# A hybrid attention and MLP layer: two more blocks of modulation columns as products on PE, page halves on ACT, and the last two fillers in one generator

## The chip, the cores and the metric

The kernel runs on one core of one Trainium2 chip. The metric is the device time of one execution in microseconds (us). The engines are named as in the profile: PE (TensorE, matrix products; PEld is its weight load), DVE (VectorE), ACT (ScalarE), POOL (GpSimd), SP (SyncE, which issues the DMAs here).

## The reference

One layer over 1024 rows of 1024 columns, in float32. A conditioning vector c gives six rows of 1024 (shift, scale and gate of two sub-layers); the mixer runs two attention groups beside each other, and an MLP with a causal convolution follows.

```python
mod = jnp.dot(jax.nn.silu(c), w_ada[l]) + b_ada[l]
sh_a, sc_a, g_a, sh_m, sc_m, g_m = jnp.split(mod, N_MOD, axis=-1)
h = modulate(rmsnorm(x, g_attn_norm[l]), sh_a, sc_a)
proj = jnp.dot(h, w_in[l])                       # q latent 256, kv latent 128, rope key 32, 3 x 512
q = jnp.dot(rmsnorm(q_lat, ...), w_q_up[l])      # 8 heads of 96
kv = jnp.dot(rmsnorm(kv_lat, ...), w_kv_up[l])   # 8 heads of 64 + 64
o_mla = mla_attention(q, k, v)                   # chunk-causal, after QK norm and rotary
o_ca = chunk_attention(cq, ck, cv, rel_bias[l])  # 9-chunk key band, 8 heads of 64
mixed = jnp.dot(jnp.concatenate([o_mla, o_ca], axis=-1), w_out[l])
x = x + g_a[:, None, :] * mixed
h = modulate(rmsnorm(x, g_mlp_norm[l]), sh_m, sc_m)
u = causal_dwconv(jnp.dot(h, w_up[l]), conv_w[l], conv_b[l])
gate, val = jnp.split(u, 2, axis=-1)
x = x + g_m[:, None, :] * jnp.dot(jax.nn.silu(gate) * val, w_down[l])
```

## The kernel before

Every product of two float32 matrices is made of three products of halves: each operand is split into a high part (a rounded copy, `hi_of`, L77) and a low part (the difference, `lo_of`, L86), and `gemm3` (L206) adds high × high, high × low and low × high in PSUM (L211 to L213). A page is a tile that holds a high and a low half.

**The opening (L298 to L513).** The eight row blocks of x are loaded, normalised in place on DVE (L371), and then for each of the eight column blocks d four things happen (loop at L483). The weights of the query and key columns of the first head pair are loaded and split (`load_wk`, L229; ACT and POOL), as are some of the value weights. The scale and the shift of block d, 128 columns each, are computed into `modT`: for d below NPE = 2 as sixteen products with one moving column (L495: the stationary operand is a 128 × 128 piece of w_ada, the moving one a column of silu(c)), for the other six as two reductions over 1024 elements on DVE (L504). The w_ada pages of `load_ada` (L304) rotate through five tiles (`wa`). `mod_transpose` (L456) transposes the block for the row halves h = 0 and h = 1 on PE (L463), and writes the modulated page (d,h). For h = 0 ACT writes the high half straight from PSUM (L468) and a float32 copy `hv` (L469), and POOL the low half; for h = 1 ACT writes `hv`, POOL casts the high half from it (L83), and DVE makes the low half (L87). Last, `gemm3` adds block d to the query and key columns of the first head pair for the eight row blocks, in four PSUM banks (`qk`).

**The attention part.** There are 32 units: 16 of chunk attention (head pair p = 0 to 3, head o, row half g; named c with p and o), then 16 of latent attention (head group gr = 0 and 1, head hh, row half g; named m with gr and hh). The loop at L1189 writes each unit's blocks of scores, exponentials and value products, and between them the preparation of the next units (`prep`, transposes of their query and key pages) and fillers: other PE work, cut into small steps by generators. `fillers` (L1131) is a list worked from the front: value columns, query and key columns of head pairs 1 to 3, value columns, the latent columns (`f_m`), `f_up(0)` and `f_up(1)` (queries, keys and values of the two latent head groups from the latents), and `f_oca` (the output projection of the chunk-attention columns, 16 tiles with n = column half and t = row block). `pace` (L1178) calls `fill_step` (L1141) until the filler cost spent so far reaches a line through the points `knots` over the attention cost so far; a step of `f_up` is counted UP_W = 3.2 times. A unit's `need` names fillers that have to be finished before its `prep`: every latent unit of group gr needs all of `up{gr}`, because `prep` (L1109) transposes four row blocks of q and k, and the unit works on both. `f_oca` waits until the first latent unit's value products begin (`ca_done`).

`f_up_steps` (L753) takes the row blocks t = 0 to 7 in turn: a query product of 384 columns (tile `qu`), its copy and squares on ACT, a key and value product of 512 columns (tile `ku`), and for each second t the norms and rotary steps on ACT, DVE and POOL (`rope_apply`, L696). The products of `f_up`, `f_oca` and the other fillers share two PSUM banks, tag `mm`.

The weights of the output projection are prepared by `wo_steps` (L847): a load of 128 × 256, a product with the gate row on POOL (L860, the gate row is the tile `gabc`), and a split on ACT and POOL. `first_wo` (L876) loads the gate row into a tile of the tag `pg` and prepares the first four row blocks for n = 0; its steps are called from `f_up(1)` after its eighth step. The attention columns of a row block are loaded in `f_oca` into `cl` and split into `ch` and `cl`, tiles of the tag `R` (five, shared with the raw tiles of `f_up`).

A scheduler of the tile framework then puts all instructions of each engine in an order by its own estimate of times; `tc.issue_after` ties an instruction behind another. The engines work through that order one instruction after another. SP issues every DMA, in order.

**After the attention.** The output projection of the latent columns (tile `op`), the norm, and the MLP: up-projections with seven instead of eight products of blocks (L1325 to L1327), convolution, the g tiles to memory, and the down-projection (L1567 to L1569), which PE fills.

## Time and profile before

| | us |
|---|---|
| median of 3 runs (1393.77 to 1395.97) | 1395.44 |
| the profiled execution | 1393.72 |
| its span, first to last instruction | 1391.5 |
| PE busy | 1295.8 (93%) |
| DVE busy | 1029.7 (74%) |
| ACT busy | 817.3 (59%) |
| POOL busy | 745.1 (54%) |
| mean granted clock of PE | 0.962 |

Times inside the trace count from the start of the span. The granted clock is the share of full speed that the throttle gave PE; in this trace it is 1 or 0.5, and a mean between them is a share of time. A row of the timeline has its start, its duration, the engine, the line, the operation, the tiles written and read, and in brackets the idle time of the engine just before and what ended it. A row of the waits has the total, the number and the longest. Rows of a tile give the shortest, the median and the longest duration in ns, and the first and the last start.

| what | when, us |
|---|---|
| last query and key product of the opening | 69 |
| first chunk unit's products | 87 |
| last chunk unit's output written | 413 |
| first and last latent unit's output written | 431, 645 |
| up-projections of both groups | 357 to 474 |
| output products of the chunk columns | 491 to 639 |

### The profile page before, as it was taken

How to read it: one execution, taken by the hardware profiler on the slowest of the kernel's cores; microseconds unless marked ns; L12 is line 12 of the kernel's file. 1: busy time of each engine (PE TensorE's matmuls, PEld its weight loads, DVE VectorE, ACT ScalarE, POOL GpSimd, SP SyncE). 2: the span in 40 equal slices, each digit the busy share in tenths (PEclk: the TensorE clock that was granted, in tenths of full speed). 3: DMA queues.
4: the chain of work that ended last, by engine and by line, in shares of the span. 5: the costliest groups of instructions: out<-in, count | busy, mean ns of one | idle time of the engine just before them, and what ended most of it. 6: DMA issues, size and time to landing. Idle time of an engine off the chain costs nothing.

```text
span 1391.5 us, 20573 instructions
## 1 busy us (share of the span) xinstructions
PE 1295.8 (93%) x7140; PEld 884.3 (64%) x7140; DVE 1029.7 (74%) x1512; ACT 817.3 (59%) x1584; POOL 745.1 (54%) x844
## 2 busy tenths in 40 slices
PE   8888999999878899997989989999999979999998
PEld 7877788878545466555844434444444438888887
DVE  7758887776668867674679989888888875566564
ACT  5646676566778767664786566666666533333331
POOL 5844434244453572443533876666666626666563
PEclk7999999999979899998999999999999989999999
DMA  9412333222000243225516422222211006446443
GB/s 352 135 39 79 100 100 96 79 77 62 24 23 20 59 142 96 87 95 183 214 46 234 144 98 92 91 91 92 82 71 61 31 31 219 151 144 244 163 145 106
DMA packets 85764, 153.06 MB, mean 110 GB/s; under 512 B 8854, under 2 KB 49050, under 8 KB 85660
## 3 DMA queue, kind: packets, MB, share of 16 engines
q1 hardware_dynamic: 85660, 151.75, 32.6%
q8 instruction: 56, 0.92, 0.3%
q14 instruction: 48, 0.39, 0.1%
HBM read 122.88 MB, written 28.84 MB: 109 GB/s over the span
## 4 chain that ended last, share of the span: by engine, by line
PE 68%; DVE 12%; ACT 6%; POOL 5%; issue 5%; DMA 4%; SPq 0%; POOLq 0%; ACTq 0%; DVEq 0%
PE p L1326 8%; PE p L1325 8%; PE p L1327 8%; PE dn L1567 6%; PE dn L1568 6%; PE dn L1569 6%; PE tm L1045 3%; PE tc L1045 1%; DMA aw<-w_ada 1%; PE op L211 1%; DMA x<-x 1%; PE op L213 1%; PE op L212 1%; PE oc L211 1%; PE pvm L1072 1%
## 5 line engine op out<-in xcount | busy, mean ns | idle before, releaser
L87 POOL TENSOR_TENSOR wds<-wd,wds 128x512 fp32r<-128x512 f32 x88 | 152.4, 1752 | 104.2 <-ACT wds L81 104.1
L1567 PE MATMUL dn<-wds,g 128*128 128x512 f32 x352 | 136.8, 395 | 9.1 <-ACT g L81 9.1
L81 ACT ACTIVATE wds<-wd 128x512 fp32r<-128x512 f32 x88 | 54.7, 624 | 152.4 <-PE dn L1569 152.4
L1568 PE MATMUL dn<-wds,g 128*128 128x512 f32 x352 | 136.7, 391 | 0.0
L1554 DVE TENSOR_TENSOR wd<-wd,gmbc 128x1024 f32<-128x1024 f32 x44 | 73.8, 1680 | 84.1 <-DMA wd<-w_down 84.1
L1569 PE MATMUL dn<-wds,g 128*128 128x512 f32 x352 | 135.3, 389 | 0.0
L1056 DVE TENSOR_TENSOR hlm<-pm,hlm 128x512 f16<-128x512 f32 (+1 forms) x96 | 64.6, 682 | 35.7 <-POOL hlm L83 22.4
L1406 ACT ACTIVATE u<-c,pk,wcv 128x1024 f32<-128x1024 f32 x44 | 52.2, 1232 | 51.1 <-DVE c L1446 43.9
L1567 PEld LDWEIGHTS dn<-wds,g 128*128 128x128 f32 x352 | 67.1, 191 | 23.7 <-ACT g L81 9.6
L87 DVE TENSOR_TENSOR g<-gr,g 128x512 fp32r<-128x512 f32 x44 | 71.0, 1614 | 6.7 <-ACT g L81 6.4
L1568 PEld LDWEIGHTS dn<-wds,g 128*128 128x128 f32 x352 | 66.6, 189 | 13.7
L1045 PE MATMUL tm<-qt,kt 96*128 96x512 f16 (+7 forms) x288 | 69.6, 338 | 6.0 <-ACT hlm L1053 2.4
L1569 PEld LDWEIGHTS dn<-wds,g 128*128 128x128 f32 x352 | 66.1, 188 | 13.8
L83 POOL TENSOR_SCALAR hlm<-pm 128x384 f16<-128x384 f32 (+2 forms) x48 | 25.2, 525 | 92.4 <-PE pvm L1074 44.7
L1407 DVE SCALAR_TENSOR_TENSOR u<-c,wcv,u 128x1023 f32<-128x1023 f32 x44 | 56.0, 1308 | 24.4 <-ACT u L1406 24.4
L1049 ACT ACTIVATE pm<-tm,scm 128x512 f32<-128x512 f32 (+1 forms) x96 | 55.2, 580 | 31.4 <-PE tm L1045 24.0
L1056 DVE TENSOR_TENSOR hlc<-pc,hlc 128x256 f16<-128x256 f32 (+3 forms) x96 | 52.1, 547 | 22.5 <-POOL hlc L83 11.7
L1045 PEld LDWEIGHTS <-kt 128*128 128x128 f16 (+2 forms) x480 | 45.7, 100 | 34.9 <-issue 16.9
L1049 ACT ACTIVATE pc<-tc,sca 128x512 f32<-128x512 f32 (+3 forms) x96 | 50.3, 525 | 29.9 <-DVE hlc L1056 13.4
L1002 DVE TENSOR_REDUCE mz<-sm 128x1 f16<-128x128 f32 (+3 forms) x64 | 48.2, 753 | 20.4 <-PE sm L1000 17.3
L81 ACT ACTIVATE wd<-wu 128x512 f16<-128x512 f32 x22 | 13.9, 630 | 83.6 <-DVE wu L1337 83.6
L1318 POOL TENSOR_TENSOR wa<-wu,wa 128x512 f16<-128x512 f32 x22 | 35.4, 1609 | 50.3 <-ACT wa L81 50.1
(470 smaller groups left out, 4551.0 us busy)
## 6 DMA issues: line engine op xcount, KB each, us to landing
wu<-w_up SPq DMA_DIRECT2D x44, 512.0 KB, 4.0
wd<-w_down SPq DMA_DIRECT2D x44, 512.0 KB, 3.6
aw<-w_ada SPq DMA_DIRECT2D x96, 128.0 KB, 2.2
g_d<-u SPq DMA_DIRECT2D x22, 512.0 KB, 2.6
gr<-g_d SPq DMA_DIRECT2D x44, 256.0 KB, 3.0
adaw<-w_ada_a SPq DMA_DIRECT2D x16, 512.0 KB, 6.8
x<-x SPq DMA_DIRECT2D x8, 512.0 KB, 7.5
wq_r<-w_qk SPq DMA_DIRECT2D x32, 128.0 KB, 2.4
```

The source lines that it names most:

```text
L81: return act.activation(o, i, AF.Copy)
L87: return (pool if eng == "p" else dve).tensor_tensor(o, i, f32(hi), op=SUB)
L1045: last = pe.matmul(s[:, c0:c1], l, m, start=(y == 0), stop=(y == len(todo) - 1))
L1049: recent["a"] = act.activation(p[:, :w], s[:, :w], AF.Exp, scale=ninv)
L1056: lo = recent["v"] = dve.tensor_tensor(hl[:, 1, :w], p[:, :w], hl[:, 0, :w], op=SUB)
L1325: pe.matmul(pt, sh, pg[:, 0], start=(k == 0), stop=False)
L1326: pe.matmul(pt, sh, pg[:, 1], start=False, stop=False)
L1327: pe.matmul(pt, sl, pg[:, 0], start=False, stop=(k == 3))
L1554: dve.tensor_tensor(raw[:], raw[:], gmbc[:], op=MUL)
L1567: pe.matmul(pts[t][n], sh, w[n][:, 0], start=(j == 0), stop=False)
L1568: pe.matmul(pts[t][n], sh, w[n][:, 1], start=False, stop=False)
L1569: pe.matmul(pts[t][n], sl, w[n][:, 0], start=False, stop=(j == NF - 1))
```

## The change

Four things change.

- **Modulation columns.** The blocks whose columns are products on PE are PE_D = (0, 1, 4, 6) instead of 0 and 1; their pages of w_ada are laid out on the host for it. Blocks 4 and 6 no longer use the DVE reductions. The first product of such a block is tied behind the last transpose of the block before.
- **Page halves.** The high half of the pages with h = 1 is written by ACT from PSUM, as for h = 0, instead of being cast by POOL.
- **Fillers.** `f_up(1)` and `f_oca` become one generator, `f_mix`. Once chunk attention is over (`ca_done`), each turn calls one step of the preparation of the output weights, until the first four row blocks are ready; from then on turns alternate between the two. Before that, and once `f_oca` is over, turns go to `f_up(1)`. A latent unit with g = 0 needs only the first four row blocks of its group (`up{gr}a`). The step weights are 3.2 for `f_up(0)` and 2.0 for `f_up(1)`. The knots ask for the fillers up to `f_up(0)` by the 13th chunk unit instead of the 14th, and for half of the mixed work after six latent units, where it was all of `f_up(1)` and a fifth of `f_oca`.
- **Tiles.** The six value tiles of chunk attention get tags, and serve again behind it: two for the halves of the gate row (which leaves the tag `pg`), two for `cl`, two for `ch` (which leave `R`). The split of the next row block stands behind the first of the two steps of an output product, its load behind the second. The first preparation of weights takes two parts in a step.

```diff
-NPE, ROPE_0 = 2, 9
+PE_D, ROPE_0 = (0, 1, 4, 6), 9
-O_EARLY = 0.2
-UP_W = 3.2
+MID = 0.5
+UP_W = (3.2, 2.0)
...
-                pe.transpose(pt[:, j * P:(j + 1) * P], src(j), ident[:])
+                last_lo["tr"] = pe.transpose(pt[:, j * P:(j + 1) * P], src(j), ident[:])
...
-        if d < NPE:
+        if d in PE_D:
...
-                    last_lo["pm"] = pe.matmul(pm[:, i:i + 1], wada[2 * d + i][:, k * P:(k + 1) * P], cs[:, k:k + 1],
-                              start=(k == 0), stop=(k == ND - 1))
+                    with tc.issue_after(last_lo["tr"].ins) if d > 1 and i + k == 0 else nullcontext():
+                        last_lo["pm"] = pe.matmul(pm[:, i:i + 1], wada[2 * d + i][:, k * P:(k + 1) * P], cs[:, k:k + 1],
+                                                  start=(k == 0), stop=(k == ND - 1))
...
-                                     hw, "hT", st, 16, "ap"[h], "pv"[h])
+                                     hw, "hT", st, 16, "a", "pv"[h])
...
+            if t == 4:
+                done.add(f"up{gr}a")
...
     def f_up(gr):
-        steps_in[0] = 0
         for c in f_up_steps(gr):
-            yield c * UP_W
-            steps_in[0] += gr
-            if steps_in[0] > 8 * gr and gr:
-                next(wo_next[0], None)
+            yield c * UP_W[gr]
...
+    def over_v(i, name, dt=F32):
+        return at.tile([P, 768], dt, name=name, tag=f"vca{i}", bufs=1)[:, :512]
...
-        gab.append(pgtile([P, D], F32, "gabc"))
-        sp.dma_start(gab[0][:], ga_d[:])
-        yield from wo_steps(4, 0)
+        for n in range(2):
+            gab.append(over_v(n, f"gabc{n}"))
+            sp.dma_start(gab[n], ga_d[:, n * 512:(n + 1) * 512])
+        yield from wo_steps(4, 0, 2)
...
+    def f_mix():
+        gens = {"up1": f_up(1), "oca": f_oca()}
+        prepared, turn = False, 0
+        while gens:
+            if ca_done and not prepared:
+                prepared = next(wo_next[0], 1) is not None
+            turn += 1
+            if "up1" in gens and ("oca" not in gens or not prepared or turn % 2):
+                key = "up1"
+            elif prepared:
+                key = "oca"
+            else:
+                yield None
+                continue
+            c = next(gens[key], None)
+            if c is None:
+                gens.pop(key)
+                done.add(key)
+            else:
+                yield c
...
-        u.need = [f"up{gr}"]
+        u.need = [f"up{gr}" + ("" if g else "a")]
...
-               ("m", f_m()), ("up0", f_up(0)), ("up1", f_up(1)), ("oca", f_oca())]
+               ("m", f_m()), ("up0", f_up(0)), ("mix", f_mix())]
...
-    W_IN, W_M, W_UP, W_O = 21.0e3, 36.4e3, 13.0e3 * UP_W, 41.5e3
-    W_A = 5 * W_IN + W_M + W_UP
+    W_IN, W_M, W_UP, W_O = 21.0e3, 36.4e3, 13.0e3, 41.5e3
+    W_A = 5 * W_IN + W_M + W_UP * UP_W[0]
+    W_B = W_UP * UP_W[1] + W_O
-    knots = [(0.0, INIT * W_IN), (14 * C_CA, W_A), (16 * C_CA + 6 * C_M, W_A + W_UP + O_EARLY * W_O),
-             (16 * C_CA + 16 * C_M, W_A + W_UP + W_O), (1e9, 1e9)]
+    knots = [(0.0, INIT * W_IN), (13 * C_CA, W_A), (16 * C_CA + 6 * C_M, W_A + MID * W_B),
+             (16 * C_CA + 16 * C_M, W_A + W_B), (1e9, 1e9)]
```

41 lines of the change are left out of this document (23 added, 18 removed).

## The prediction

> **What bounds the kernel now.** I read the page first: the busy share of each engine, the slices, and the chain that ended last.
>
> ```profile
> span 1391.5 us, 20573 instructions
> PE   8888999999878899997989989999999979999998
> PEclk7999999999979899998999999999999989999999
> PE 68%; DVE 12%; ACT 6%; POOL 5%; issue 5%; DMA 4%; SPq 0%; POOLq 0%; ACTq 0%; DVEq 0%
> ```
>
> PE carries 68% of the chain, so time comes from PE's idle stretches and from its granted clock. The execution took 1393.72 us, 2.2 more than its span; the median of the runs shown is 1395.44, 1.7 above it. I make the sum against 1393.72 and add 1.7 at the end. The change touches two places: the opening (until about 77 us) and the handover from chunk attention to latent attention (about 341 to 540 us). So next I asked for the busy time of the engines by stretch: PE is the first figure after the width, ACT the fourth, PEclk the granted clock.
>
> ```profile
> core 0: us, PE busy (x) PEld busy (x) DVE busy (x) ACT busy (x) POOL busy (x), PEclk, DMA share, GB/s
> 19.50:27.00 7.50, 7.50 (x36) 7.50 (x36) 4.36 (x5) 5.57 (x9) 5.14 (x8) 0.50 1.02 362
> 24.00:45.00 21.00, 16.56 (x113) 15.82 (x111) 18.89 (x26) 10.04 (x21) 15.53 (x13) 0.83 0.92 320
> 45.00:77.00 32.00, 32.00 (x248) 32.00 (x249) 23.52 (x46) 22.76 (x58) 26.91 (x44) 0.91 0.24 74
> 160.00:300.00 140.00, 136.50 (x1070) 118.51 (x1070) 107.09 (x240) 87.80 (x216) 49.42 (x87) 1.00 0.32 91
> 341.00:413.00 72.00, 55.87 (x311) 38.62 (x310) 47.87 (x122) 57.58 (x157) 40.42 (x87) 0.86 0.10 27
> 413.00:540.00 127.00, 115.15 (x680) 74.48 (x679) 97.05 (x168) 95.28 (x220) 67.73 (x106) 0.93 0.26 76
> 540.00:640.00 100.00, 91.54 (x527) 56.27 (x525) 64.97 (x97) 61.71 (x115) 35.06 (x46) 0.95 0.27 86
> ```
>
> From 24 to 45 DVE is busy 18.9 of 21 us and PE waits; from 45 to 77 PE never waits, so there every product added is paid. From 160 to 300 PE is full at clock 1.00. From 341 to 540 PE is idle 16.1 + 11.9 = 28.0 us, and its clock takes 55.87 × 0.14 + 115.15 × 0.07 = 15.9 us more: 44 us lost in 199. From 540 to 640 the same sum is 8.5 + 4.6 = 13 us in 100. The handover is the richest place.
>
> **The opening, part by part.** Now the two waits of PE, with what DVE did ahead of the second, and the groups that change.
>
> ```profile
> 35.78 0.39 PE L211 MATMUL qk<-wq_s,hT 128*128 128x256 f32 x1 [1.14 <-POOL hT L83]
> 44.98 0.58 PE L213 MATMUL qk<-wq_s,hT 128*128 128x256 f32 x1 [3.15 <-DVE hT L87]
> 42.49 1.82 DVE L504 CUSTOM_DVE_ANT_0 adaw<-adaw,csb,pk 128x1024 f32<-128x1024 f32 x1
> 44.25 0.68 DVE L87 TENSOR_TENSOR hT<-hv,hT 128x512 fp32r<-128x512 f32 x1
> L504 DVE CUSTOM_DVE_ANT_0 adaw<-adaw,csb,pk 128x1024 f32<-128x1024 f32 x6 | 9.2, 1540 | 0.0
> L504 DVE CUSTOM_DVE_ANT_0 adaw<-adaw,csb,bsc 128x1024 f32<-128x1024 f32 x6 | 8.9, 1490 | 0.7 <-DMA adaw<-w_ada_a 0.7
> L83 POOL TENSOR_SCALAR hT<-hv 128x512 fp32r<-128x512 f32 x8 | 7.0, 875 | 3.7 <-ACT hv L469 3.7
> L468 ACT ACTIVATE hT<-ht_ps,modT 128x512 fp32r<-128x512 f32 x8 | 6.2, 772 | 5.3 <-DVE modT L499 2.7 <-PE ht_ps L463 2.6
> ```
>
> The low half of page (2,1) stood on DVE behind the reductions of blocks 4 and 5; that is the 3.15 us. Blocks 4 and 6 leave DVE: 2 × (1.54 + 1.49) = 6.1 us less there. The eight POOL casts (7.0 us) go, and ACT gets eight more page halves of 0.77 = 6.2 us; ACT is busy 10 of 21 us and 23 of 32, so they lie beside PE's work. I take both waits as gone: **−1.1 − 3.2 = −4.3**. The clock of 0.91 from 45 to 77 follows the long wait; without it 32 × 0.09 = **−2.9**.
>
> Added on PE: 32 one-column products, each with a weight load. The trace records each in two (16 in the code of one block are 32 here), so 64 records. What one costs is bounded by these rows:
>
> ```profile
> 11.35 5.17 PE L495 MATMUL ada_ps<-cs,adaw 128*128 128x1 f32 x32
> 19.48 3.58 PE L495 MATMUL ada_ps<-cs,adaw 128*128 128x1 f32 x16 [0.33 <-DMA adaw<-w_ada_a]
> 47.07 0.41 PE L211 MATMUL qk_s<-wq_s,hT 128*128 128x256 f32 x1
> 47.28 0.41 PE L212 MATMUL qk_s<-wq_s,hT 128*128 128x256 f32 x1
> 57.11 0.28 PE L211 MATMUL qk_s<-wq_s,hT 128*128 128x256 f32 x1
> 57.23 0.28 PE L212 MATMUL qk_s<-wq_s,hT 128*128 128x256 f32 x1
> 32.40 0.60 PE L463 MATMUL ht_ps<-ident,x 128*128 128x128 f32 x4
> ```
>
> At half clock one record takes 3.58/16 = 0.22, the mixed row 5.17/32 = 0.16. A 256-column product steps by 0.21 slow (47.07 to 47.28) and 0.12 fast (57.11 to 57.23): the same pace as a one-column record when slow, so I take 0.12 when fast too. 64 × 0.12 = **+7.7**. Lower end 0, if all fell into waits; upper end 64 × 0.22 = 14.1. No gain is possible from the products themselves.
>
> A new wait: block 4's columns now come from PE. In the built order the last four of its products stand directly ahead of the transposes of block 4, and the products on page (4,0) follow; they wait for two small DVE operations and an ACT half (0.77), and the second page's half is the third on ACT. Behind them all of PE waits: **+2.0**, between 0 and 4. For block 6, 18 value products stand in between and cover it (18 × 0.12 = 2.2). Buffers: block 6's and 7's loads reuse tiles that PE now frees some microseconds later, and SP is in order, so the query weights behind them are late by as much; 55 value products (30 before) now stand ahead of the last query product and cover that. Opening: −4.3 − 2.9 + 7.7 + 2.0 = **+2.5**.
>
> One rule speaks against this half. The row first: from 19.5 to 27 PE was busy 7.50 of 7.50 us, with one-column products and transposes, at clock 0.50. The Trainium skill, page "TensorE: Matmul & The Clock Gate", Part 1, says that the clock is set by how busy the array was in free-running windows of 3.4 us, and Part 4 that transposes do not count as busy; the trace agrees for transposes and one-column products alone. By that rule mixed stretches may be slow too; what that would cost is the third rival, from rows.
>
> **The handover, part by part.** The filler work itself is the same; only its place and pace change. Its rows, PE's waits from 308 to 540 and then from 540 to 640:
>
> ```profile
> L211 PE MATMUL qu<-wq,latT x32: 331/342/667, 357.5 to 466.8; 128*128 128x384 f32 x32
> L211 PE MATMUL oc<-wo,ch x64: 390/398/774, 491.3 to 639.2; 128*128 128x512 f32 x64
> L860 POOL TENSOR_TENSOR wor<-wor,gabc x32: 721/731/1629, 446.1 to 663.4; 128x256 f32<-128x256 f32 x32
> PE mq_ps L935 <- POOL qn L707: 4.7, 2, 3.5
> PE sm L988 <- DVE mz L1002: 3.1, 6, 0.7
> PE ku L211 <- ACT uqr L794: 2.7, 2, 2.4
> PE ku L211 <- DVE vm L602: 2.3, 2, 1.9
> ...
> PE tm L1045 <- ACT hlm L1053: 2.4, 2, 1.7
> PE mrm_ps L1010 <- DVE mz L1002: 2.0, 2, 1.6
> PE sm L988 <- DVE mz L1002: 1.6, 2, 0.9
> 480.00:490.00 10.00, 6.62 (x27) 3.53 (x27) 6.45 (x14) 6.77 (x21) 7.86 (x15) 0.66 0.28 81
> ```
>
> Before, all up-projection work lies between 357 and 474 and the dense output products start only at 491. In the built order of the change the first up-projection begins one unit earlier (inside chunk unit 2,1), its second half follows more slowly, and the first output product stands at the end of latent unit 0,1 instead of in unit 0,2. The two fillers hardly alternate: the second up-projection is nearly over when the output products begin.
>
> - **First latent page.** It now waits for half of the up-projection. From the last product that it needs to its last transpose there are 27 products before, 71 after: 44 × 0.12 to 0.21 = 5 to 9 us more cover for a wait of 4.7 in all. −4.7.
> - **Up-projection products waiting for their PSUM bank** (2.7 + 2.3): fewer in a row per unit, so I take −3.0 of 5.0.
> - **Attention's own waits** (sm, mrm, tm and the like) are as dense from 540 to 640, 8.5 us of idle in 100, where output products stand between. Nothing is taken for them.
> - **Clock.** 15.9 us lost; with the idle falling from 28.0 to 20.3 I take a third, −5.3.
> - **Output weights.** Their chain (gate row, load, POOL, ACT, POOL) was late before: 480 to 490 shows 3.4 us of idle at clock 0.66. It now starts on chunk attention's value tiles, free only after the last chunk unit, and is due about one unit sooner. I keep the price as it was, 0; if it is later still, or the loads of the attention columns that now share those tiles are, PE stands behind the first output product, and latent attention with it: up to another 3.4 + 6.6 × 0.34 = 5.6.
>
> Handover: −4.7 − 3.0 − 5.3 = **−13.0**, between 0 (or +5.6) and −9.7 − 15.9 = −25.6. Where idle goes, ACT is next: 57.58 of 72 us in the first stretch, so this stretch can't fall by more than some 12 us. The stages behind 650 us keep their order and are put at nothing. Sum: 1393.72 + 2.5 − 13.0 = 1383.2; with 1.7, **1385**.
>
> **The rivals.**
> - **All of it comes**: the handover runs at the losses of 540 to 640. Its work of 155 us at 13% loss takes 178, −21; opening 0 to +2.5: **1375**. For it: the fillers are more even. Against: ACT's 80%. Chance 0.12.
> - **It doesn't do what it says**: the turns do not happen, and the chain of output weights, started no sooner, comes late. Only the first page's −4.7 remains, +3.4 for the late weights, +2.5: **1396.6**. For it: the built order and the row of 480 to 490. Chance 0.18.
> - **The other side: half clock in the opening.** Between the first product of block 4 and the last of block 6 stand 64 one-column records, 80 query products and 16 transposes (0.60 for four): 7.7 + 9.6 + 2.4 = 19.7 us, of which only the 9.6 count as busy if the rest doesn't. At half clock it takes 64 × 0.10 + 80 × 0.09 + 2.4 = 16.0 more. Opening +18.5, handover −13: **1401**. It decides once about two thirds of that stretch run at half clock (10.6 of the 16.0). For it: the row of 19.5 to 27. Against: the products are interleaved with dense ones in groups of two to sixteen records. Chance 0.20.
>
> **How the numbers follow.** Forecast (1385, own range 1377 to 1392) 0.50, the rivals 0.12, 0.18 and 0.20. A measurement of this kernel can tell 0.2%, 2.8 us. Faster: 0.50 + 0.12 + 0.04 of the second rival = 0.66. Within: 0.11 of the second and 0.02 of the third = 0.13. Slower: 0.21. The range of 1374 to 1401 leaves out half of the first rival and half of the third, 0.16; the far ends of the single bounds need all of them at once.
>
> **What would show it.** Right: no PE wait over 1 us for a page at 35 to 45 us; 64 more one-column records 0.12 apart; the wait for mq_ps under 1 us; idle from 341 to 530 near 20 us and clock above 0.93; the second half of the kernel starting some 10 us earlier. Wrong: a granted clock of 0.5 around the products of blocks 4 and 6; PE waiting for wo or cl at the first output product; ACT over 90% in the handover with PE as idle as before.

## The result and the profile after

The changed kernel takes 1409.99 us (median of 4 runs, 1408.39 to 1412.69) against 1395.5 before: 1.0106 times as long, with a 95% interval of 1.0090 to 1.0122. It is slower by 14.5 us, outside the range that was forecast and on its other side. The profiled execution took 1410.12, its span is 1408.3; that is 16.8 more than the span of before. First the page of the changed kernel: its span, PE's busy slices and granted clock, and the chain by engine.

```profile
span 1408.3 us, 20665 instructions
PE   9898999998878899987988989999999979999998
PEclk7999999999899999998999999999999999999999
PE 64%; DVE 11%; ACT 8%; DMA 6%; POOL 6%; issue 5%; SPq 0%; POOLq 0%; ACTq 0%; DVEq 0%
```

PE is still the bound, but its share of the chain fell from 68 to 64%, and ScalarE and the DMAs have more of it. To see where the 16.8 us are, I cut both spans at the same work: the first score product of chunk attention, the first output product of the stage behind attention, and the last of these. Four stretches result: the opening, attention, the output stage, and the rest. These are the windows of before (width, PE busy, then the other engines, granted clock, DMA share):

```profile
0.00:87.30 87.30, 77.33 (x514) 69.93 (x515) 65.50 (x171) 51.15 (x110) 61.22 (x99) 0.86 0.59 207
87.30:650.90 563.60, 506.79 (x3376) 378.90 (x3376) 405.55 (x835) 380.91 (x893) 239.66 (x409) 0.95 0.25 76
650.90:699.70 48.80, 48.79 (x220) 40.16 (x221) 27.40 (x39) 30.34 (x53) 26.61 (x37) 0.96 0.64 238
699.70:1391.50 691.80, 662.85 (x3034) 395.36 (x3032) 531.24 (x469) 354.90 (x529) 417.59 (x300) 0.99 0.34 117
```

And these are the same four of the changed kernel:

```profile
0.00:99.50 99.50, 88.97 (x597) 81.12 (x598) 55.05 (x168) 56.93 (x119) 54.41 (x93) 0.86 0.52 182
99.50:661.20 561.70, 499.40 (x3359) 371.70 (x3357) 400.94 (x832) 381.16 (x894) 239.58 (x410) 0.96 0.26 76
661.20:716.80 55.60, 52.13 (x220) 41.67 (x221) 30.70 (x39) 29.73 (x52) 25.46 (x35) 0.90 0.56 206
716.80:1408.30 691.50, 662.50 (x3034) 395.25 (x3032) 529.64 (x469) 354.31 (x529) 419.29 (x300) 0.99 0.34 117
```

The opening is 12.2 us longer, attention 1.9 shorter, the output stage 6.8 longer, the rest 0.3 shorter: 16.8 in all. The forecast had +2.5, −13 and 0 for the first three.

**The opening.** VectorE was relieved as foreseen: from 45 to 77 us it is busy 8.3 of 32 us instead of 23.5. These are the windows of the changed kernel at the stretches of the forecast:

```profile
24.00:45.00 21.00, 20.86 (x138) 20.03 (x137) 15.98 (x22) 14.93 (x30) 14.24 (x13) 0.77 0.86 305
45.00:77.00 32.00, 27.96 (x227) 27.51 (x225) 8.32 (x26) 16.98 (x37) 12.96 (x15) 0.95 0.20 62
341.00:413.00 72.00, 56.19 (x339) 39.71 (x338) 49.78 (x121) 57.52 (x156) 33.13 (x77) 0.91 0.16 43
413.00:540.00 127.00, 110.19 (x654) 70.55 (x652) 95.75 (x179) 99.04 (x234) 72.16 (x119) 0.96 0.20 60
```

PE no longer waits from 24 to 45 us (20.86 of 21 busy), but it is idle 4.0 us from 45 to 77, where it never waited before. The timelines of PE, VectorE and ScalarE at that place (start, length, then the idle time ahead of the instruction and its releaser in brackets):

```profile
53.48 0.39 PE L211 MATMUL qk_s<-wq_s,hT 128*128 128x256 f32 x1 [3.88 <-ACT hT L468]
```

```profile
45.77 1.28 DVE L505 CUSTOM_DVE_ANT_0 adaw<-adaw,csb,bsc 128x1024 f32<-128x1024 f32 x1 [1.73 <-DMA adaw<-w_ada_a]
...
49.18 1.39 DVE L505 CUSTOM_DVE_ANT_0 adaw<-adaw,csb,pk 128x1024 f32<-128x1024 f32 x1 [1.92 <-PE ht_ps L463]
...
50.50 0.21 DVE L498 SCALAR_TENSOR_TENSOR modT<-ada_ps,bsc,pk 128x1 f32<-128x1 f32 x1
```

```profile
51.95 0.42 ACT L246 ACTIVATE wv_j<-wv_r 128x256 f32<-128x256 f32 x1 [1.26 <-DMA wv_r<-w_v]
...
52.67 0.76 ACT L468 ACTIVATE hT<-ht_ps,modT 128x512 fp32r<-128x512 f32 x1
```

The wait is that of page (4,0). Block 4's last product had ended by 48.7, but the two small VectorE operations that combine its columns (L498 and the next) stand behind the two reductions of block 7 and start at 50.50. (The profile puts the second reduction's idle time down to transposes, which it doesn't read. Its page was issued at 43.94 and loads of these pages took 3.8 to 5.1 us here, so a late load is likelier.) Then ScalarE's page half stands behind value weights, one of which waited 1.26 us for its load, and starts at 52.67. On engines that run in order, operations that nobody needs yet made PE wait. The Trainium skill, page "TensorE: Matmul & The Clock Gate", Part 1, says that the queues of VectorE and ScalarE are strictly first in, first out; the trace agrees, with the 1.8 us between 48.7 and 50.5.

The added records cost what was forecast, or a little less:

```profile
41.23 1.40 PE L496 MATMUL ada_ps<-cs,adaw 128*128 128x1 f32 x12
42.49 0.36 PE L211 MATMUL qk_s<-wq_s,hT 128*128 128x256 f32 x1
```

From 41.23 to 42.49 pass 1.26 us for 12 records, 0.105 each; 64 make 6.7. Of the other 5.5 us of the opening, 2.2 are value products done earlier (175 records instead of 157 ahead of the first score product, 0.12 each), 0.6 more idle time (99.5 − 88.97 = 10.5 against 10.0), and 88.97 × 0.14 − 77.33 × 0.14 = 1.6 clock; about 1 us is left to the rounding of the clock.

The half clock did move, though. Before, it lasted from about 13 to 30 us and from 44 to 51. In the changed kernel it lasts from 13 to 33.5 us, from 54 to 57.5 behind the wait for page (4,0), and from 88 to 91.5 behind a wait of 3.0 us for value columns just ahead of the chunk units. That last wait was 2.1 us before, with no half clock behind it. The row of the changed kernel behind it:

```profile
87.60:91.40 3.80, 3.46 (x17) 3.50 (x18) 3.19 (x8) 1.08 (x3) 3.80 (x5) 0.58 0.03 10
```

**The handover.** By the windows above, 341 to 540 us has 15.8 + 16.8 = 32.6 us of idle time (28.0 before, 20.3 forecast), and its clock takes 56.19 × 0.09 + 110.19 × 0.04 = 9.5 us (15.9 before, 10.6 forecast). The clock did what was forecast, the idle time went the other way. These windows hold other work than before, since the changed kernel is some 12 us late here: shifted by 12 us, 353 to 552, the idle time is 29.2 us and the clock takes 8.9. Over all of attention the idle time grew by 5.5 us (56.8 to 62.3), the clock took 5.4 less (506.79 × 0.05 against 499.40 × 0.04), and 2.0 is the value products done in the opening: that is the 1.9 by which attention got shorter. The waits of PE over all of attention, before and after (total, times, longest), say which. The rows of mq_ps and ku of before stand in the prediction.

```profile
PE sc L988 <- DVE mz L1002: 6.8, 5, 2.9
...
PE tc L1045 <- ACT hlc L1053: 2.6, 3, 1.1
...
PE pvc L1073 <- DVE hlc L1056: 0.8, 3, 0.3
PE tc L1045 <- ACT pc L1049: 0.6, 1, 0.6
```

```profile
PE tc L1071 <- ACT pc L1075: 6.3, 6, 3.0
PE sc L1014 <- DVE mz L1028: 5.5, 8, 1.4
PE pvc L1099 <- DVE hlc L1082: 4.5, 8, 1.0
PE tc L1071 <- ACT hlc L1079: 4.3, 6, 1.1
PE mq_ps L961 <- POOL qn L708: 3.2, 2, 1.9
PE ku L211 <- ACT uqr L797: 2.7, 4, 0.9
...
PE ku L211 <- ACT wk L81: 1.1, 1, 1.1
```

The waits that were to go fell only in part: the page wait from 4.7 to 3.2, the bank waits of ku from 5.0 to 2.7, and a new wait of 1.1 us for weights of ku came (the row with wk). But chunk attention's own waits grew. The rows shown went from 10.8 to 20.6 us; all rows of sc, tc and pvc together, the small ones included, from 14.2 to 22.6. Latent attention's (sm, tm and pvm) went from 15.9 to 18.6. The chunk units did not get less filler by count: up to the last value product of chunk attention PE has 1074 records of filler products (value, query, key and latent columns, up-projections) before and 1057 after, and nearly all of the difference is the value products done in the opening. So it is the place of the filler among the units that differs; which place makes which wait isn't shown.

**The output stage.** The change edits nothing there, and yet it takes 6.8 us more: 3.5 idle, the rest clock behind it. The rows of PE and ScalarE of the changed kernel, and ScalarE's of before at the same place:

```profile
688.40 0.50 PE L211 MATMUL op<-wo,oh 128*128 128x512 f32 x1 [2.88 <-ACT oh L81]
```

```profile
684.60 2.19 ACT L1342 ACTIVATE wu<-wu,wss 128x1024 f32<-128x1024 f32 x2 [2.58 <-POOL wss L1337]
686.69 0.61 ACT L81 ACTIVATE wa<-wu 128x512 f16<-128x512 f32 x1
687.21 0.61 ACT L81 ACTIVATE wb<-wu 128x512 f16<-128x512 f32 x1
687.73 1.13 ACT L81 ACTIVATE oh<-ol 128x512 fp32r<-128x512 f32 x2
```

```profile
673.35 1.14 ACT L81 ACTIVATE oh<-ol 128x512 fp32r<-128x512 f32 x2
674.39 2.18 ACT L1313 ACTIVATE wu<-wu,wss 128x1024 f32<-128x1024 f32 x2
```

Before, the casts of the next output tiles (oh) stood ahead of the scaling of the next stage's first weights (wu). After, the order is reversed: ScalarE waits 2.58 us for GpSimd with the scaling, and the casts, whose data have long landed, stand behind it. PE waits 2.88 us for them.

### The profile page after: what moved, and what is told of

Same layout as the page of the kernel before. It is cut to its first block, busy times and chain, and to the rows that moved or that the text cites. A ratio compares the mean times of both kernels' runs of the same rounds, so it can differ in the third digit from the quotient of the medians.

```text
span 1408.3 us, 20665 instructions
## 1 busy us (share of the span) xinstructions
PE 1303.0 (93%) x7204; PEld 889.7 (63%) x7204; DVE 1016.3 (72%) x1506; ACT 822.1 (58%) x1592; POOL 738.7 (52%) x836
## 4 chain that ended last, share of the span: by engine, by line
PE 64%; DVE 11%; ACT 8%; DMA 6%; POOL 6%; issue 5%; SPq 0%; POOLq 0%; ACTq 0%; DVEq 0%
PE p L1354 8%; PE p L1355 8%; PE p L1356 8%; PE dn L1596 6%; PE dn L1597 6%; PE dn L1598 6%; DMA wor<-w_out 2%; PE tm L1071 2%; PE tc L1071 2%; POOL wo L87 1%; PE op L213 1%; PE op L211 1%; PE op L212 1%; PE ipq L211 1%; DVE mz L1028 1%
## 5 line engine op out<-in xcount | busy, mean ns | idle before, releaser
L1583 DVE TENSOR_TENSOR wd<-wd,gmbc 128x1024 f32<-128x1024 f32 x44 | 70.3, 1602 | 83.8 <-DMA wd<-w_down 83.8
L1082 DVE TENSOR_TENSOR hlm<-pm,hlm 128x512 f16<-128x512 f32 (+2 forms) x96 | 64.1, 675 | 30.3 <-POOL hlm L83 15.9
L1598 PEld LDWEIGHTS dn<-wds,g 128*128 128x128 f32 x352 | 66.1, 188 | 13.6
L1082 DVE TENSOR_TENSOR hlc<-pc,hlc 128x512 f16<-128x512 f32 (+3 forms) x96 | 50.6, 532 | 28.8 <-ACT hlc L1079 15.9
L1071 PEld LDWEIGHTS <-kt 128*128 128x128 f16 (+2 forms) x480 | 45.8, 100 | 33.8 <-issue 13.8
L1071 PE MATMUL tc<-qt,kt 128*128 128x512 f16 (+3 forms) x192 | 55.7, 313 | 10.7 <-ACT pc L1075 6.3
L81 ACT ACTIVATE wd<-wu 128x512 f16<-128x512 f32 x22 | 13.8, 629 | 82.3 <-DVE wu L1366 82.3
L1028 DVE TENSOR_REDUCE mz<-sm 128x1 f16<-128x128 f32 (+3 forms) x64 | 48.2, 753 | 17.1 <-PE sm L1026 14.1
```

What stands on the lines that cost most here:

```text
L81: return act.activation(o, i, AF.Copy)
L1071: last = pe.matmul(s[:, c0:c1], l, m, start=(y == 0), stop=(y == len(todo) - 1))
L1082: lo = recent["v"] = dve.tensor_tensor(hl[:, 1, :w], p[:, :w], hl[:, 0, :w], op=SUB)
L1583: dve.tensor_tensor(raw[:], raw[:], gmbc[:], op=MUL)
L1598: pe.matmul(pts[t][n], sl, w[n][:, 0], start=False, stop=(j == NF - 1))
```

## The experiments

The theory after this reading: three separate parts that add up, namely the opening (records, and a wait made by queue order), a handover that gives back what it gains, and an output stage put in another order. The main rivals: later work takes up the late opening and the fillers carry the loss (A); and the output stage is slow because attention ends in another state (B).

All results in one table: the ratio to the kernel before on the same chip with its 95% interval, what that ratio makes of 1396 as a difference in us, and the lengths of the four stretches in the profiled execution, cut as above.

| kernel | ratio (interval) | us | opening | attention | output stage | rest |
|---|---|---|---|---|---|---|
| before | 1 | 0 | 87.3 | 563.6 | 48.8 | 691.8 |
| after | 1.0106 (1.0090 to 1.0122) | +14.8 | 99.5 | 561.7 | 55.6 | 691.5 |
| open_alone | 1.0056 (1.0043 to 1.0069) | +7.8 | 102.4 | 559.0 | 49.6 | 692.4 |
| open_queue | 1.0027 (1.0014 to 1.0041) | +3.8 | 98.8 | 558.5 | 48.5 | 692.5 |
| open_double | 1.0059 (1.0043 to 1.0075) | +8.2 | 104.8 | 555.0 | 49.2 | 691.1 |
| half_alone | 0.9948 (0.9931 to 0.9964) | −7.3 | 87.0 | 560.6 | 48.2 | 691.5 |
| block6_only | 0.9961 (0.9947 to 0.9974) | −5.4 | 89.9 | 556.7 | 48.9 | 691.7 |
| fill_alone | 1.0043 (1.0027 to 1.0059) | +6.0 | 88.8 | 559.4 | 58.7 | 692.9 |
| fill_ordered | 1.0056 (1.0037 to 1.0075) | +7.8 | 89.2 | 563.7 | 53.4 | 698.0 |
| fill_old_tiles | 0.9971 (0.9959 to 0.9983) | −4.0 | 87.9 | 563.0 | 49.2 | 692.3 |
| after_ordered | 1.0090 (1.0073 to 1.0107) | +12.6 | 99.3 | 562.0 | 49.4 | 697.5 |
| after_old_tiles | 1.0105 (1.0086 to 1.0124) | +14.7 | 99.0 | 570.5 | 49.9 | 693.5 |
| after_no_block4 | 1.0147 (1.0130 to 1.0163) | +20.5 | 89.1 | 571.2 | 61.4 | 692.2 |
| half_fill_gate | 1.0049 (1.0036 to 1.0062) | +6.8 | 88.3 | 571.8 | 49.3 | 692.4 |
| half_fill_old | 1.0029 (1.0019 to 1.0039) | +4.0 | 87.4 | 570.7 | 48.5 | 694.7 |
| turns_old_pace | 0.9998 (0.9986 to 1.0009) | −0.3 | 86.9 | 563.9 | 48.9 | 691.6 |
| new_pace | 1.0022 (1.0008 to 1.0037) | +3.1 | 88.9 | 569.1 | 48.6 | 691.9 |

The stage lengths are those of one execution, which can lie some 3 us off the median: 1393.08 against 1396.48 for turns_old_pace, and the execution of before (1393.72) is 1.8 to 3.3 faster than its own medians beside the other kernels.

### The two parts by themselves: open_alone, fill_alone

open_alone is the kernel before with the opening's edits only:

```diff
-NPE, ROPE_0 = 2, 9
+PE_D, ROPE_0 = (0, 1, 4, 6), 9
...
-                                     hw, "hT", st, 16, "ap"[h], "pv"[h])
+                                     hw, "hT", st, 16, "a", "pv"[h])
```

> The opening part alone (blocks 4 and 6 as products, both page halves by ACT), with the fillers of before. Theory (three separate parts that add up): the 64 added one-column records are paid (+7.4) and one new wait of 3.9 us for block 4's page stands where two waits of 4.3 stood, so the first chunk unit starts 10 to 12 us later and nothing gives that back: 1405 to 1407 us, +10 to +12 on before. Rival A (the later work has slack and takes the delay up, the loss of the change comes from the fillers): within 4 us of before. The output stage has the order of before on ScalarE, so it should take 48.8 us from its first to its last product, as before.

Measured 1404.05, +7.8, less than the theory's 10 to 12 and more than rival A's 4. The opening took 102.4 us, 15.1 more than before, with the same wait of 3.9 us for page (4,0), attention 4.6 less than before, the output stage 49.6. So the late opening costs half or more of its delay, a part is taken up later, and rival A falls as the main cause.

fill_alone is the changed kernel with the old opening:

```diff
-PE_D, ROPE_0 = (0, 1, 4, 6), 9
+PE_D, ROPE_0 = (0, 1), 9
...
-                                     hw, "hT", st, 16, "a", "pv"[h])
+                                     hw, "hT", st, 16, "ap"[h], "pv"[h])
```

> The fillers alone (the two last ones in turn, new knots, new tiles), with the opening of before. Its output stage is built with the same ScalarE order as the changed kernel: the scaling of the first weights of the next stage ahead of the casts of tiles 4 to 6. Theory: attention about -2, output stage +6 to +7, so +4 to +5 on before: about 1399.5. Rival A (the fillers carry the loss): +14 or more, 1409. Rival B (the output stage's extra time came from the late opening, not from this order): -2, 1393.

Measured 1401.37, +6.0, a little above the theory's 4 to 5 and far below rival A; the output stage took 58.7. The two parts add up: 7.8 + 6.0 = 13.8 beside the measured 14.8.

### The order in the output stage: after_ordered, fill_ordered, after_old_tiles, fill_old_tiles

In after_ordered and fill_ordered the scaling is held back by hand until tile 6 is cast. The same edit moves more: the first splits of these weights go from tile 3 to tile 6, and the preparation of the next pair from tile 4 to tile 6.

```diff
+    def scale_wu(j):
+        with behind(o_hi.get(6)):
+            for i in range(2):
+                act.activation(raws[j][i][:], raws[j][i][:], AF.Copy, scale=wu_t[j][:, 2:3])
...
+        if t == 6:
+            scale_wu(0)
             gens[0] = ff_w(0)
             w0 = [next(gens[0]) for _ in range(2)]
-        if t == 4:
             gens[0] = iter(list(gens[0]))
             scale_ff(1, ps2.tile([P, 512], F32, name="wss_ps1", tag="hT", bufs=2))
+            scale_wu(1)
```

> The changed kernel with one edit in the output stage: the scaling of the first weights of the next stage is issued behind the cast of tile 6, as it stood in the kernel before. Theory: the fifth output product no longer waits for its cast (2.9 us) and the half clock behind that wait goes too, so the output stage falls from 55.6 to about 49 us and the time from 1410.0 to about 1403. Rival B (that stage is slow because attention ends in another state, weights and clock): the time stays at 1408 or above.

> The fillers alone, with the same edit in the output stage. Theory: only the handover is left, -2 on before: about 1393.5, between 1391 and 1396. Rival A: 1403 or more. If the forecast of the handover had been right and the opening had spoiled it (another start of the chunk units gives another order), it would show here: 1382.

Measured 1409.62 and 1405.36; the theory had about 1403 and 1393.5, and missed both. In after_ordered the output stage fell to 49.4, as expected, so it was not the state at attention's end that made it slow (rival B's reason), but the rest grew by 6.0, most likely because the next stage's weights were now prepared later. In fill_ordered the stage fell only to 53.4: PE still waited 3.0 us for a cast, which stood behind a square on ScalarE that had itself waited 4.8 us for VectorE. Holding the scaling back moved the loss on, so these two don't settle the price. after_ordered shows only that the stage itself can lose its 6 us this way.

after_old_tiles and fill_old_tiles put the gate row and the attention columns back on their old tiles, and nothing else; that restores the old order without a tie by hand:

```diff
-        for n in range(2):
-            gab.append(over_v(n, f"gabc{n}"))
-            sp.dma_start(gab[n], ga_d[:, n * 512:(n + 1) * 512])
+        g_ = pgtile([P, D], F32, "gabc")
+        sp.dma_start(g_[:], ga_d[:])
+        gab.extend([g_[:, :512], g_[:, 512:]])
...
-                cl[i] = over_v(2 + i % 2, f"cl{t}_{n}", F32R).rearrange("p (k t) -> p k t", k=4)
...
+                cl[i] = rtile(f"cl{t}_{n}", (P, 4, P), F32R)
...
-                ch[i] = over_v(4 + i % 2, f"ch{t}_{n}", F32R).rearrange("p (k t) -> p k t", k=4)
...
+                ch[i] = rtile(f"ch{t}_{n}", (P, 4, P), F32R)
...
```

> The changed kernel with one thing undone: the gate row, the attention columns and their upper halves stand on the tiles that they had before, not on the value tiles of chunk attention. In the built order ScalarE casts output tiles 4 to 6 ahead of the scaling of the next stage's first weights again, as before. Theory (the new places set other memory free, so these weights come earlier and their scaling is put ahead of the casts): the output stage takes 48.8 to 49.5 us, the next stage keeps its 445.8, and the time falls from 1410.0 to about 1403.5, the opening's +10 less 2. Rival A (the loss moves on with the attention's end, as when the scaling alone was held back): 1408 or more. Rival B (the old places cost the handover something): the attention stage over 566 us.

> The fillers in turn with the new knots, but with the old tiles, and the opening of before. Theory: opening 87.3 to 89, attention 560 to 564 (the handover gains 0 to 4 of the 13 that were forecast), output stage 49: 1391 to 1396, no slower than before. Rival (the new tiles were what made turns possible, without them the output weights come late): 1398 or more.

In both, ScalarE has the casts first again, the output stage takes 49.9 and 49.2, and the rest stays within 2 us of before. fill_old_tiles is 4.0 faster than before, 10.0 faster than fill_alone. after_old_tiles gains nothing in all (1412.57): attention takes 570.5 instead of 561.7, as rival B of that run had it. Up to the middle of latent unit 0 its PE order is that of the changed kernel, and there it was already 3.6 us later (first ku product at 372.0 instead of 368.4), which is then a difference between two executions; the first output product came 8.5 later (487.1 against 478.6), so about 5 us belong to the old tiles. Over all kernels the stage goes by this order: 55.6, 58.7 and 61.4 us in the three with the scaling first, 48.2 to 49.9 in the twelve, the kernel before among them, in which one or more of the casts stand first without a hand on them. That the new tiles bring the reversed order is shown; by which freed memory or modelled moment is not. half_fill_gate below puts back the gate row alone and has a cast first too (49.3), so the gate row's place is the likelier cause of the two.

### What the opening's cost is made of: open_queue, half_alone, block6_only, open_double

open_queue mends the two orders of the opening alone:

```diff
-                wv0.append(load_wk("wv0_", I["w_v"][0], k, 256, ssw=ssw0))
...
+                with tc.issue_after(last_lo["hv"].ins) if d > 4 else nullcontext():
+                    wv0.append(load_wk("wv0_", I["w_v"][0], k, 256, ssw=ssw0))
...
-                dve.tensor_tensor_reduce(w[:], w[:], csb[:], 1.0, init, MUL, ADD, accum_out=o)
+                with tc.issue_after(last_lo["c4"].ins) if d == 7 else nullcontext():
+                    dve.tensor_tensor_reduce(w[:], w[:], csb[:], 1.0, init, MUL, ADD, accum_out=o)
```

> The opening part alone, with two orders set by hand: VectorE combines block 4's columns ahead of the two reductions of block 7, and ScalarE casts the later value weights behind block 4's page. Theory: the wait of 3.9 us for page (4,0) is made of the reduction of block 7 whose load landed late (1.6) and of value weights whose loads were awaited (1.9); it falls under 1.5 us, and the time falls by 2.5 to 4 from the opening alone (1404.0): 1400 to 1401.5. What is left over before, +4.5 to +6, is the price of the 64 one-column records less the removed waits. Rival (the wait is the chain product, combination, ScalarE itself): wait and time as in the opening alone.

Measured 1400.03. PE's wait for page (4,0):

```profile
50.40 0.39 PE L211 MATMUL qk_s<-wq_s,hT 128*128 128x256 f32 x1 [0.91 <-ACT hT L468]
```

The wait fell from 3.9 to 0.9 us and the time by 4.0 (+7.8 to +3.8). So the order of the queues made the wait, and the chain from product to page costs under 1 us.

half_alone is the kernel before with one argument changed, `"ap"[h]` to `"a"` (all page halves by ScalarE).

> Only the page halves by ScalarE, blocks 4 and 6 still on VectorE, old fillers. Theory: the wait of 1.1 us for a cast on GpSimd goes, the one of 3.2 us behind VectorE's reductions stays: -1, between -2 and 0: about 1395, not to be told from before. Rival (ScalarE is in the way of pages or value weights): +2 or more.

Measured 1389.86: −7.3, the fastest kernel of the study, and much more than either theory said. The two waits of 1.1 and 3.2 us became four of 0.8 to 0.9, and no half clock follows them in the opening. In this profile the opening is only 0.3 shorter and attention 3.0; a part of the difference is the fast execution of before that the stages are compared with, and where the rest of the gain lies isn't shown.

block6_only takes half_alone and moves block 6 to PE, `PE_D = (0, 1, 6)`.

> Of the opening part only block 6 as a product (32 records) with both page halves by ScalarE, old fillers. Theory (each one-column record is paid in a full PE, the rest of the opening's loss is clock around them): between the halves alone (1389.9) and the two blocks with the queues mended (1400.0): 1394 to 1396. Rival (VectorE's relief is worth something once the waiting block is gone): 1390 or less.

Measured 1390.5, +1.9 on the halves alone, and the two intervals overlap: close to the rival. By themselves block 6's 32 records cost next to nothing. So of the 15.1 us by which both blocks worsen the halves (+7.8 against −7.3), block 4 adds 13.2 on top of block 6: 4.0 for the queues, 9.2 without them. No kernel has block 4 alone. The opening of open_queue is 8.9 us longer than that of block6_only; 32 × 0.105 = 3.4 are records. Most of the rest is clock. First open_queue, then block6_only, in the same stretch:

```profile
53.40:56.80 3.40, 3.40 (x17) 3.40 (x17) 0.45 (x1) 2.17 (x6) 3.40 (x4) 0.50 0.22 70
56.80:60.20 3.40, 3.40 (x32) 3.40 (x31) 0.69 (x1) 2.69 (x8) 1.60 (x3) 1.00 0.14 46
60.20:67.00 6.80, 6.80 (x34) 6.80 (x34) 0.00 (x0) 0.00 (x0) 0.09 (x1) 0.50 0.14 41
```

```profile
60.20:67.00 6.80, 6.80 (x59) 6.80 (x59) 1.90 (x10) 4.46 (x9) 3.83 (x4) 1.00 0.13 40
```

From 53.4 to 67.0 open_queue has PE busy without a gap, and in 10.2 of these 13.6 us the clock is 0.50: 34 records in 6.8 us where block6_only does 59 at full clock. That is 5.1 us, and 3.4 + 5.1 = 8.5 of the 8.9. The first 3.4 us of half clock follow a stretch in which PE had waited (50.0 to 53.4, busy 2.00 of 3.40). The 6.8 us from 60.2 follow none: the stretch ahead of them was full, and most of it was one-column products, those of block 6. The same products had full clock in block6_only, so this part of the price seems to belong to the two blocks together and to where the clock's windows fall. The record has a direct comparison: open_alone and the changed kernel have the same order on PE from 24 to 98 us, but open_alone was at half clock behind block 6's products and the changed kernel was not, and its opening took 2.9 us longer (102.4 against 99.5). First open_alone, then the changed kernel:

```profile
63.10:69.90 6.80, 6.80 (x35) 6.80 (x35) 0.03 (x1) 0.00 (x0) 0.00 (x0) 0.52 0.01 2
```

```profile
64.20:67.60 3.40, 3.40 (x32) 3.40 (x31) 0.83 (x6) 1.39 (x3) 0.00 (x0) 1.00 0.00 0
```

In the 3.4 us ahead of these spells, one-column products took 2.33 us in open_queue and 2.26 in open_alone, and half clock followed; in the changed kernel they took 2.09 and full clock followed. Three cases are too few to call that a threshold. The Trainium skill, page "TensorE: Matmul & The Clock Gate", Part 1, says that windows of some 3.4 us run freely and that activity in them sets the clock. The free windows agree: the edges lie at other places of the work in each execution. That being busy is enough does not agree here, unless one-column products hardly count.

open_double makes every product of blocks 4 and 6 twice, the second time into columns that nobody reads:

```diff
-            for i in range(2):
+            for c in (range(2) if d < 2 else (2, 3, 0, 1)):
+                i = c % 2
```

> The opening with the queues mended, and every product of blocks 4 and 6 made twice (the second time into columns that nobody reads, which is more work than the reference needs): 64 more records. Theory (a record costs its 0.115 us and no more): +7.4 on 1400.0, 1407.4. Rival (one-column products do not keep the clock up, so that they make their neighbours slow): 64 x 0.22 and some 3.4 us of half clock: 1412 to 1418. Rival (they fall into waits): 1400 to 1403.

Measured 1404.43, +4.4 on open_queue, between the theory (7.4) and the rival that they fall into waits. PE was idle 4.3 us less in the opening (98.8 − 90.42 = 8.4 against 104.8 − 100.70 = 4.1), while the opening grew by 6.0. A one-column record is paid, but not where PE would have waited. The rival by clock has a part in it too: between 47 and 75 us half clock lasted 17.0 us, against 10.2 in open_queue.

### Parts put together, and pace against turns: half_fill_gate, half_fill_old, new_pace, turns_old_pace, after_no_block4

half_fill_gate and half_fill_old were to be the best of all: the halves, blocks 4 and 6 on VectorE, the new fillers, and the old tile for the gate row, or the old tiles for the columns too.

> A version put together from the parts that helped: page halves by ScalarE (blocks 4 and 6 on VectorE), fillers in turn, gate row on its old tile, attention columns on the value tiles. Theory (parts add up: -5.6 for the halves against the record of before, -3 for the fillers with the output stage in order): 1386 to 1389, below all kernels so far. Rival (the fillers gain nothing): 1390 or more.

> The same with the attention columns on their old tiles too. Theory: output stage as before, the first output product some 3 to 5 us later than with the columns on the value tiles: 1388 to 1392. Rival (the place of the columns does not matter): as the other.

Measured 1403.1 and 1401.03, slower than before. The halves (−7.3) and the fillers with old tiles (−4.0) do not add up: together +4.0. The loss is in attention, 571.8 and 570.7 us with 69.7 and 67.6 of them idle, against 560.6 with 55.3 in half_alone. This left open which part of the new fillers costs, so pace and turns were parted on top of the halves. new_pace has the old fillers and the new costs and knots; turns_old_pace is half_fill_gate with the old ones:

```diff
-MID = 0.5
-UP_W = (3.2, 2.0)
+MID = 0.6005
+UP_W = (3.2, 3.2)
...
-    knots = [(0.0, INIT * W_IN), (13 * C_CA, W_A), (16 * C_CA + 6 * C_M, W_A + MID * W_B),
+    knots = [(0.0, INIT * W_IN), (14 * C_CA, W_A), (16 * C_CA + 6 * C_M, W_A + MID * W_B),
```

> As the version half_fill_gate (halves by ScalarE, fillers in turn, 1403.1), but with the old pace: filler costs 3.2 and 3.2, the knots of before. Theory (the new pace, which gives the chunk units less filler and moves it into the latent units, opens waits there as large as those it closes): back near the halves alone, 1389 to 1393, with idle in the attention stage near 55 instead of 69.8. Rival (taking turns, or the half-need, is what costs): 1400 or more.

> Halves by ScalarE and the old fillers, one after the other, but with the new costs and knots. Theory (pace alone costs): 1398 to 1404, idle in the attention stage 65 or more. Rival (turns cost): 1389 to 1392, as the halves alone.

Measured 1396.48 and 1398.83. The attention rows of half_alone, turns_old_pace and new_pace, in this order, each cut once more at the last value product of chunk attention (first chunk attention, then latent attention):

```profile
87.00:408.40 321.40, 292.97 (x2130) 241.83 (x2129) 229.13 (x552) 217.95 (x544) 131.41 (x249) 0.96 0.24 69
408.40:647.60 239.20, 212.29 (x1236) 135.18 (x1236) 170.40 (x283) 163.12 (x348) 107.46 (x158) 0.94 0.28 85
```

```profile
86.90:404.80 317.90, 289.15 (x2130) 240.85 (x2128) 228.54 (x551) 217.02 (x544) 130.64 (x249) 0.97 0.25 72
404.80:650.80 246.00, 214.57 (x1238) 136.37 (x1237) 174.89 (x283) 164.77 (x349) 108.32 (x158) 0.93 0.26 80
```

```profile
88.90:412.40 323.50, 289.97 (x2129) 238.34 (x2128) 232.89 (x550) 214.78 (x542) 129.51 (x249) 0.98 0.24 69
412.40:658.00 245.60, 214.25 (x1238) 136.50 (x1237) 168.75 (x284) 165.56 (x352) 108.63 (x160) 0.92 0.27 84
```

Against the halves alone the pace costs 10.4 us, taking turns 7.0, and both 14.1. The turns come with the columns' new tiles and with the half-need: a latent unit of the first row half asks for only half of its up-projection. new_pace came out as its theory said; turns_old_pace fell between its theory and its rival. The waits of PE tell the two apart: under the new pace those of chunk attention (all rows of sc, tc and pvc) make 23.2 us, as in the changed kernel (22.6); with turns at the old pace they make 11.5, as in the halves alone (12.0), and the page wait of mq_ps, which the half-need was to shorten, is 5.3 against 4.0.

But in these executions the price is not where these waits are. Chunk attention is only 2.1 us longer under the new pace, and 3.5 shorter with turns; all three kernels have 1064 records of filler products in it. Latent attention is 6.4 and 6.8 us longer, 4.4 and 4.5 of it idle time, the rest a lower clock; that is more than the 3 us or so by which executions differ, though not by much. And fill_old_tiles has the new pace too, with chunk waits of 24.1 us, and is 4.0 us faster than before. So the new pace opens the chunk waits, as shown; why it is dear on top of the new page halves and not on top of the old ones stays open.

after_no_block4 is the changed kernel with `PE_D = (0, 1, 6)`:

> The changed kernel with block 4 back on VectorE; block 6, halves, fillers and tiles as in the change. Theory (block 4 alone makes the opening late: its page waits 3.9 us, its 32 records cost 3.7, and the half clock around it 5): 12 to 14 less than 1410.0, 1396 to 1398. Rival (in the changed kernel the late opening is taken up later, the fillers carry the loss): 1404 or more.

Measured 1416.26, 6 us slower than the changed kernel: the rival's side (1404 or more), far from the theory's 1396 to 1398. Its chunk attention, latent attention and output stage:

```profile
89.10:411.70 322.60, 289.50 (x2118) 238.67 (x2116) 234.20 (x550) 215.08 (x543) 129.96 (x250) 0.97 0.24 72
411.70:660.30 248.60, 214.70 (x1238) 136.52 (x1237) 168.31 (x284) 165.84 (x353) 107.91 (x160) 0.92 0.26 79
660.30:721.70 61.40, 54.36 (x227) 43.79 (x228) 31.93 (x40) 30.20 (x54) 25.78 (x35) 0.88 0.50 186
```

Its opening is 10.4 us shorter than that of the changed kernel, but attention took 9.5 more and the output stage 5.8 more. Nearly all of the 9.5 lie behind chunk attention: latent attention took 239.3 us in the changed kernel. So here an early opening was all lost again. The four kernels with the new pace and the new page halves whose opening ended at 87.4 to 89.1 us need 569.1 to 571.8 for attention; the changed kernel and after_ordered, whose opening ended at 99.5 and 99.3, need 562, though after_old_tiles, at 99.0, needs 570.5. An early start alone does not do this: fill_alone, fill_ordered and fill_old_tiles start at 87.9 to 89.2 us with the new pace and the old page halves, and need 559.4 to 563.7. What does it, among the orders of instructions that come with the page halves and the start, stays open. Rival A is right to this extent, that within the changed kernel block 4's cost isn't added on top: the parts' prices hold on the kernel before, and three attempts to take a part out of the changed kernel (after_ordered, after_old_tiles, after_no_block4) won nothing clear.

## Why the prediction was wrong, step by step

The forecast was +2.5 for the opening, −13.0 for the handover and nothing behind it. The stages measured +12.2, −1.9 (all of attention), +6.8 and −0.3.

- **"I take both waits as gone: −1.1 − 3.2 = −4.3."** They went, but a wait of 3.9 us took their place, and the opening's idle time is the same (10.0 before, 10.5 after). The step that failed is the new wait, "+2.0, between 0 and 4": it stands at the edge of its bounds, and by another mechanism. I counted the chain behind the product; that chain costs 0.9 (open_queue). I looked at PE's built order and not at VectorE's or ScalarE's, where operations for later blocks stood ahead.
- **Clock of the opening, −2.9.** It did not come: +1.6 here. The half clock behind the old wait went, and came back behind the wait for page (4,0), behind the wait ahead of the chunk units, and for one more spell of 3.4 us at the start. The wait was not the only reason for half clock: 6.8 us of it in open_queue have no wait ahead.
- **64 records, +7.7.** Right: 6.7 in the span.
- **Half clock in the opening, the rival of +16.** Right in kind and too large: 5.1 us in open_queue, 3.4 of it without a wait ahead. In the changed kernel it did not come: around the products of blocks 4 and 6 only the wait for page (4,0) had half clock behind it. That looks like luck in where the clock's windows fell: open_alone, with the same order, was at half clock there.
- **SP's loads and the value products cover each other.** Right for the query weights. But the value products that stood between the pages before (first at 36 us) now come only after the last waits (66 us), so nothing covers the wait for page (4,0).
- **Page halves, "so they lie beside PE's work".** Mis-sized: alone they are worth −7.3, and the two blocks hide that: +15.1 on top of them.
- **Handover, −13.0.** The largest miss. The page wait fell by 1.5 instead of 4.7, the bank waits by 2.3 instead of 3.0 (with a new wait of 1.1 for weights beside them), the clock by 6.4 (5.3 forecast). The failed step is "Attention's own waits … Nothing is taken for them": the same amount of filler, placed by a new pace, left the chunk units' waits 8.4 us longer and latent attention's sm, tm and pvm 2.7, so that attention's idle time grew by 5.5 where 7.7 were to go in the handover. new_pace shows that pace alone opens the chunk waits. What the pace costs in all depends on the rest of the kernel: 10.4 on top of the halves, while fill_old_tiles, with pace and turns, gained 4.0.
- **The output weights, 0 to +5.6.** Right: the first output product came at 478.6, behind no wait for weights.
- **"The stages behind 650 us keep their order and are put at nothing."** Wrong: +6.8, by an order that the new places of three tiles turned round. The built order shows it; the forecast read that order only around the edits.
- **The rivals.** The one on the other side (1401) had the sign, with a mechanism that gave a part of it. None had the output stage.

## What to carry to other kernels

When work moves from one engine to another, read the new order on every engine that stands between the product and its user, not on the receiving engine alone: a small operation behind a large one that nobody needs yet costs as much as the work that was moved. A new pace for the same filler moves waits as well as closing some, and what it costs can show in another stretch than the waits that it opens, so count the idle time over all the stretches that it feeds. And when tiles change places, look at the stages behind them, even where no line was edited, and test parts together as well as alone: here −7.3 and −4.0 made +4.0.

## What the runs showed of the hardware that was not expected

- PE busy without a gap was granted half clock where one-column products filled much of it: 0.50 from 60.2 to 67.0 us in open_queue, after 3.4 us at 1.00 with PE busy 3.40 of 3.40, 2.33 of them one-column products. The same order of products can have half clock in one execution and full clock in another (open_alone 0.52 from 63.1 to 69.9 us, the changed kernel 1.00 at the same products).
- Two executions with the same PE order up to there stood 3.6 us apart at the first ku product (after and after_old_tiles, 368.4 and 372.0), so a stage in one profile can't be read closer than a few us.
